# A two-layer DeltaNet and attention backbone: query norms moved to the end of the heads, the output weights' first casts moved to GpSimd, rotation rows placed behind turned blocks, and the last stage's sums read one tile later

## The chip, the cores and the metric

The kernel runs on one NeuronCore of a Trainium2 chip. The metric is the device time of one execution in microseconds (us), from the chip's own clock. PE is the matrix engine, DVE the vector engine, ACT the scalar engine, POOL the GpSimd engine, and SP the queue that issues most DMAs.

## The reference, cut to what matters

512 latent tokens and 256 context tokens of width 1024 go through two layers. Layer 0 is a gated DeltaNet in both directions with 16 value heads, 8 query/key heads and chunks of 64 tokens. Layer 1 is grouped-query attention with rotary positions. A final norm ends it.

```python
def l2_norm(x):
    return x * lax.rsqrt(jnp.sum(x * x, axis=-1, keepdims=True) + NORM_EPS)

# layer 0
qkv = jax.nn.silu(centred_dwconv(p[..., :DN_CONV_DIM], conv_w))   # p = u @ w_in
z   = p[..., DN_CONV_DIM:DN_CONV_DIM + DN_VAL_DIM]
q   = jnp.repeat(l2_norm(q), 2, axis=2)                           # its scale: the query norms
...
def step(s, xs):                                                  # the chunk scan
    v_new = u_i - w_i @ s
    o = qd_i @ s + qk_i @ v_new
    s = s * gl_i + kd_i.T @ v_new
...
y   = (rms_norm(o, o_norm_g) * jax.nn.silu(z)) @ w_out            # output weights
# layer 1
q, k = apply_axial_rope(rms_norm(q, q_norm_g)), apply_axial_rope(rms_norm(k, k_norm_g))
y = (softmax(q @ k.T * d ** -0.5) @ v * jax.nn.silu(z)) @ w_out
# end
h = h + gate * y
out = rms_norm(h, final_norm_g)
```

## The kernel before, in words

Every float32 operand of a large product is split into a high half (a cast to the type fp32r) and a low half (the operand less its high half), and a product takes three passes: high by high, low by high, high by low. A weight's cast therefore has a subtraction behind it, and PE waits for both. The stages, by the trace's clock:

- **Heads**, about 185 to 574 us. Forty slots of input columns (eight q, k pairs, then values `v` and gates `z`) go through a product, a convolution of five taps (L773) and a SiLU (L790, L792), with weights split at L744 and L747. Beside that POOL and DVE solve the triangular systems of the chunks (names `X`, `L`, `tmp`, `df`, `KQ`). The work is a list of `Piece` objects, each with an engine, a cost and a due time. A list scheduler (`written_out`) writes out the order once, when the program is built: it always takes the piece that can start first, and of those the one that is due first. A slot is `SLOT = 8.8` us and there are `N = 40`. One such piece is the **query norms**: eleven small DVE instructions of `rsqrt_steps` (L194 to L202) on the tile `rq` (128x48), the sums of squares of the queries, which the scan uses later.
- **Scan**, about 574 to 752 us. Twelve steps of four parts run as a hand-written loop over `x`; an iteration writes `products(x)`, `solve(x-1)` and `update(x-2)`. `products` has PE make `ks` from the state `S`, DVE make `r` (L1161), ACT make `o` (L1164), and POOL scale `S` (L1167) and add `o` to `O` (L1170). `solve` has PE make `pr` (L1184) from `r` and ACT copy it to `vn` (L1186). `update` has PE make `pq` (L1210) and `su` (L1218), and DVE add them to `O` (L1224) and `S` (L1232). Engines run their instructions in the order of this text, so whatever stands between two of them delays the second. At its end the loop also prepares the output product: fifteen steps that make the norm factors `fo` of the output (the list `chain`: L1086, L194 to L202, L1088), the first scaled copy of the output `so` (`out_scale`, ACT, L1282), and the split of the first output weights: `out_high` (L1267, the cast `woh`, on ACT) and `out_low` (L1274, the low half `wol`, on POOL).
- **Output product**, about 752 to 898 us: 32 units (two groups of tokens by sixteen heads), each with turned, gated and split columns and products into `po` (L1325).
- **Keys and values of layer 1**, about 898 to 945 us. `u_block(k, ...)` has PE turn a block of the normed tokens into a PSUM tile `ht` (L1449), DVE scale it in place (L1454), ACT copy it as the high half and DVE subtract for the low half `uL` (L1456). `kv_block` multiplies the halves by the weights (L1596). There are two such PSUM tiles in turn, so the PE's third `ht` waits for the first `uL`. `rope_rows` prepares the rotation rows with the norms' weights: eight DVE instructions, four of `cg` (L1652) and four of `sg` (L1653), 128x256. POOL meanwhile casts and splits weights for the next stage (`wz`, `wq`; L1565 the cast, L1566 the low half).
- **Attention**, to about 1137 us, and the **tail** to the end: the output product of layer 1 over four tiles of 128 tokens, the gate and residual (`finish_half`, L1987 and L1988), the square sums on ACT (L1989, into `ss`), the final norm (`finish_norm`, L1996 to L2000) and the store. A tile comes in two halves of 512 columns, and DVE reads the square sum of each half before it goes on.

Of the kernel before, what the change touches and what calls it, by code (L numbers as in the profile page):

```python
# [17 lines left out]
P = 128  # L18
# [68 lines left out]
def backbone(tc, a, out):  # L87
# [97 lines left out]
    def rsqrt_steps(x, mul, out=None, room=None):  # L185

        n = x.shape[1]
        rcount[0] += 1
        y, t = (rsp.tile([P, NT * VH], F32, tag=f"rs{i}", name=f"rs{i}_{rcount[0]}")[:, 0:n] for i in range(2))
        if room is not None:  # L190
            t = room
        yi = y.bitcast(I32)
        steps = [
            lambda: V.tensor_scalar(x, x, mul, EPS, ALU.mult, ALU.add),  # L194
            lambda: V.tensor_scalar(yi, x.bitcast(I32), -0.5, float(0x5F3759DF), ALU.mult, ALU.add),
        ]
        for i in range(3):
            to = (x if out is None else out) if i == 2 else y
            steps += [
                lambda: V.scalar_tensor_tensor(t, x, -0.5, y, ALU.mult, ALU.mult),  # L200
                lambda: V.tensor_tensor(t, t, y, ALU.mult),
                lambda to=to: V.scalar_tensor_tensor(to, t, 1.5, y, ALU.add, ALU.mult),  # L202
            ]
        return steps
# [828 lines left out]
    for t, due in enumerate((170, 200, 230, 260, 290, 320)):  # L1033
# [5 lines left out]
        for v in range(2):  # L1039
# [220 lines left out]
            c += m  # L1260
        zs_[n] = z

    def out_high(n):

        gi, h = units0[n]
        wh = fw.tile([P, D], F32R, tag="wh", name=f"woh{h}_{gi}", bufs=3)
        S.copy(wh, raws[n])  # L1267
        halves[n] = [wh]

    def out_low(n):  # L1270

        gi, h = units0[n]
        wl = fw.tile([P, D], F32R, tag="wl", name=f"wol{h}_{gi}", bufs=3)
        G.tensor_tensor(wl, raws.pop(n), halves[n][0], ALU.subtract)  # L1274
# [61 lines left out]
    squares = [(t, h) for t in (1, 0, 5) for h in range(VH)]  # L1336
    for x in range(50):
        if x == 47:
            out_scale(0)
        if x < 48:  # L1340
            products(x)
        if 0 <= x - 1 < 48:
            solve(x - 1)
        if x == 48:
            pt = out_gated(0)
        if x == 49:
            out_product(0, 2)
# [12 lines left out]
        if x in (28, 32, 36, 40):  # L1360
            with tc.issue_after(mark[0]):
                (out_load if x < 36 else gate_load)((x - 28) // 4 % 2)
        if x in (45, 46):
            out_high(x - 45)
        if x in (47, 48):
            out_low(x - 47)
        if x == 47:
            out_load(2)
            out_turn(0)
        if x == 48:  # L1370
            out_rest(0, pt)
            out_scale(1)
# [85 lines left out]
    def u_block(k, j, tiles, dst):  # L1458
        u_split(k, j, u_turn(k, j, tiles), dst)
# [210 lines left out]
    kr = {}  # L1670
# [231 lines left out]
    for u in range(32 + 4):  # L1902
# [33 lines left out]
        for half in range(2):  # L1936
            if piece and piece[0] is q_products:
                q_products(*piece[1:], range(half * 4, half * 4 + 4))
            elif piece:
                k0 = 4 * (u % 2) + 2 * half  # L1940
                z_products(piece[1], range(k0, k0 + 2))
            elif half == 0 and 26 <= u < 33:
                out_block(u - 26, 0, pg)
            elif half == 0 and u >= 33:
                s_all = raw(s3, 0, [[1, 3 * 512]])
                acc1 = [s_all[:, nh * 512:(nh + 1) * 512] for nh in range(2)]
                for k in ((0, 1, 2), (3, 4, 5), ())[u - 33]:
                    out_block(k, 1, acc1)
                if u == 35:
                    out_block(7, 0, pg)  # L1950
            if half == 1 and o is not None:
                q_turned(*last[1:], o)
            if u == 32 and half == 0:
                aq_c.__exit__(None, None, None)
                f2_c = tc.tile_pool(name="fo", bufs=2, side="right", reuse_waits="tile")
                f2 = f2_c.__enter__()
                fg = f2.tile([P, D], F32, tag="fg", name="fg", bufs=1)
                gate1 = f2.tile([P, 1, D], F32, tag="gate1", name="gate1", bufs=1)
                ss = f2.tile([P, 4, 2], F32, tag="ss", name="ss", bufs=1)
# [25 lines left out]
    def finish_half(t, nh, jk):  # L1985
        c = slice(nh * 512, nh * 512 + 512)
        V.tensor_tensor(jk[:, c], acc[t][nh], gate1[:, 0, c], ALU.mult)  # L1987
        V.tensor_tensor(hs[t][:, c], hs[t][:, c], jk[:, c], ALU.add)  # L1988
        S.activation(jk[:, c], hs[t][:, c], AF.Square, accum_out=ss[:, t, nh:nh + 1])  # L1989
        if nh == 0:  # L1990
            V.tensor_scalar(ss[:, t, 0:1], ss[:, t, 0:1], 1.0 / D, EPS, ALU.mult, ALU.add)  # L1991

    def finish_norm(t):

        x, y, w = (f2.tile([P, 1], F32, tag=f"fr{i}", name=f"fr{i}_{t}") for i in range(3))
        V.tensor_scalar(x, ss[:, t, 1:2], 1.0 / D, ss[:, t, 0:1], ALU.mult, ALU.add)  # L1996
        V.tensor_scalar(y.bitcast(I32), x.bitcast(I32), -0.5, float(0x5F3759DF - 0x400000), ALU.mult, ALU.add)  # L1997
        for _ in range(3):
            V.tensor_scalar(w, x, y, y, ALU.mult, ALU.mult)  # L1999
            V.tensor_scalar(y, w, 1.5, y, ALU.subtract, ALU.mult)  # L2000
        return y
# [6 lines left out]
    for t in range(4):  # L2008
        jk = f2.tile([P, D], F32, tag="jko", name=f"jko{t}")
        if t < 3:  # L2010
            for k in range((KT, 6, 0)[t], KT):
                out_block(k, t, acc[t])
            for nh in range(2):
                finish_half(t, nh, jk)
            V.scalar_tensor_tensor(jk, hs[t], finish_norm(t), fg, ALU.mult, ALU.mult)
            send(t, jk, slice(0, D), dma)
            if t == 0:
                load_hs(3)
        else:
            halves_ = [slice(0, 512), slice(512, D)]  # L2020
            hg = wp.tile([P, D], F32, tag="w", name="hg", bufs=3)
            for nh in range(2):
                for k in range(KT):
                    out_block(k, t, acc[t], (nh,))
                finish_half(t, nh, jk)
                V.tensor_tensor(hg[:, halves_[nh]], hs[t][:, halves_[nh]], fg[:, halves_[nh]], ALU.mult)  # L2026
            r = finish_norm(t)
            S.activation(hg[:, halves_[0]], hg[:, halves_[0]], AF.Copy, scale=r)  # L2028
            send(t, hg, halves_[0], nc.scalar.dma_start)
            V.tensor_scalar(hg[:, halves_[1]], hg[:, halves_[1]], r, None, ALU.mult)  # L2030
            send(t, hg, halves_[1], dma)
    written.__exit__(None, None, None)
    f2_c.__exit__(None, None, None)
    at_c.__exit__(None, None, None)
# [31 lines left out]
```

## Time and profile before

| what | value |
|---|---|
| median of 3 runs | 1188.99 us (1187.13 to 1191.74) |
| profiled execution | 1189.06 us, of which the trace's span is 1187.2 us |
| mean granted PE clock | 0.987 |
| PE busy | 1131.2 us, 95% of the span |
| DVE, ACT, POOL busy | 801.9, 721.1 and 584.0 us |

In the trace, a row of a timeline gives the start, the duration, the engine, the line, the operation, the tile written and the tiles read; the bracket at its end gives the time for which the engine stood idle before it and what ended that. A granted clock of 0.5 is half speed. Rows of a window give, per engine, the busy time, then the granted PE clock in the third place from the end.

### The profile page before, as it was taken

Reading aid. Unit: us, or ns where it says so; the run is one execution under the profiler, and the core shown is the slowest. Engines: PE = TensorE matmul, PEld = TensorE weight load, DVE = VectorE, ACT = ScalarE, POOL = GpSimd, SP = SyncE. Lnnn points to the kernel's source line nnn. Section 1 sums busy time; section 2 is a strip of 40 time slices with the busy share of each in tenths; the row PEclk is TensorE's granted clock in tenths of the full one; section 3 lists DMA queues with packets and bytes.
Section 4 is the critical chain, followed back from the end, with each engine's and each line's share of the span. In section 5 each row is a group of like instructions: output and inputs, shape, how many; then the busy total and the mean of one; then the engine's idle time right before and its main releaser. Section 6 shows DMA issues by size and latency. Waiting matters only on the chain. (4 is left out here: it accounts for less than half of the span.)

```text
span 1187.2 us, 27636 instructions
## 1 busy us (share of the span) xinstructions
PE 1131.2 (95%) x10739; PEld 919.0 (77%) x10739; DVE 801.9 (68%) x1723; ACT 721.1 (61%) x1885; POOL 584.0 (49%) x443
## 2 busy tenths in 40 slices
PE   3998999999979999999999999899999999999995
PEld 1676778888868888888666666688887889999884
DVE  2669565889898777763588888546557466667646
ACT  3343333889666873874478998785753246666721
POOL 0130004499998998441285586555744244130900
PEclk9899999999999999999999999999999999999998
DMA  9477976866549544979599996475744112101323
GB/s 332 153 240 240 298 218 187 238 165 167 147 138 284 182 133 131 292 218 286 157 257 248 248 274 162 158 224 185 241 155 134 36 54 72 36 19 54 107 71 89
DMA packets 171124, 208.72 MB, mean 176 GB/s; under 512 B 12497, under 2 KB 126322, under 8 KB 170226
## 3 DMA queue, kind: packets, MB, share of 16 engines
q1 hardware_dynamic: 150914, 195.19, 55.7%
q10 hardware_dynamic: 20080, 11.77, 3.3%
q8 instruction: 85, 1.39, 0.5%
q14 instruction: 45, 0.37, 0.1%
HBM read 166.16 MB, written 40.67 MB: 174 GB/s over the span
## 5 line engine op out<-in xcount | busy, mean ns | idle before, releaser
L1325 PE MATMUL po<-woh,y 128*128 128x512 f32 x384 | 129.3, 401 | 0.7 <-ACT y L1301 0.7
L1167 POOL TENSOR_TENSOR S<-S,glb 128x512 f32<-128x512 f32 x80 | 81.7, 1042 | 70.0 <-PE ks L1158 70.0
L1274 POOL TENSOR_TENSOR wol<-wo,woh 128x1024 fp32r<-128x1024 f32 x32 | 77.1, 2412 | 54.6 <-ACT woh L1267 51.6
L644 POOL TENSOR_TENSOR X<-X,tmp 128x62 f32<-128x62 f32 (+15 forms) x93 | 97.0, 1043 | 7.3
L773 DVE SCALAR_TENSOR_TENSOR acc_v<-g_v,cwv,acc_v 128x510 f32<-128x510 f32 (+3 forms) x128 | 78.2, 615 | 31.9 <-ACT acc_v L765 28.2
L758 PE MATMUL g_v<-uh,wh_v 128*128 128x512 f32 (+1 forms) x256 | 89.4, 349 | 6.6 <-DVE sil_z L790 6.6
L643 POOL TENSOR_TENSOR tmp<-L,X 128x62 f32<-128x62 f32 (+15 forms) x93 | 86.4, 929 | 6.8
L758 PE MATMUL g_z<-uh,wh_z 128*128 128x512 f32 (+1 forms) x256 | 88.7, 346 | 0.0
L758 PE MATMUL g_v<-ul,wh_v 128*128 128x512 f32 (+1 forms) x256 | 87.2, 341 | 0.0
L758 PE MATMUL g_v<-uh,wl_v 128*128 128x512 f32 (+1 forms) x256 | 87.0, 340 | 0.0
L758 PE MATMUL g_z<-ul,wh_z 128*128 128x512 f32 (+1 forms) x256 | 86.6, 338 | 0.4 <-issue 0.4
L758 PE MATMUL g_z<-uh,wl_z 128*128 128x512 f32 (+1 forms) x256 | 86.7, 338 | 0.0
L1325 PEld LDWEIGHTS po<-woh,y 128*128 128x128 f32 x384 | 72.3, 188 | 15.9 <-ACT y L1301 0.9
L1325 PE MATMUL po<-wol,y 128*128 128x512 f32 x192 | 75.6, 394 | 0.9 <-POOL wol L1274 0.9
L333 POOL TENSOR_TENSOR wl_k<-w_k,wh_k 128x1024 fp32r<-128x1024 f32 x8 | 19.1, 2389 | 103.8 <-ACT wh_k L332 103.8
L758 PEld LDWEIGHTS g_v<-uh,wh_v 128*128 128x128 f32 x256 | 49.2, 192 | 12.4 <-DVE sil_z L790 6.9
L1299 DVE SCALAR_TENSOR_TENSOR pt<-pt,og,z 128x128 f32<-128x128 f32 x96 | 34.4, 358 | 34.3 <-PE pt L1290 31.5
L1232 DVE TENSOR_TENSOR S<-su,S 128x512 f32<-128x512 f32 x80 | 51.5, 686 | 6.0 <-PE su L1218 3.9
L1158 PE MATMUL ks<-S,ck 128*64 128x256 f32 x352 | 55.2, 392 | 0.4 <-ACT o L1164 0.4
L758 PEld LDWEIGHTS g_v<-uh,wl_v 128*128 128x128 f32 x256 | 49.2, 192 | 5.5
L758 PEld LDWEIGHTS g_z<-uh,wl_z 128*128 128x128 f32 x256 | 48.9, 191 | 5.7 <-issue 0.5
L758 PEld LDWEIGHTS g_z<-uh,wh_z 128*128 128x128 f32 x256 | 49.0, 192 | 5.3 <-issue 0.4
(432 smaller groups left out, 3342.5 us busy)
## 6 DMA issues: line engine op xcount, KB each, us to landing
aw<-in_ada_w SPq DMA_DIRECT2D x24, 1024.0 KB, 8.3
wo<-in_dn_w_out SPq DMA_DIRECT2D x32, 512.0 KB, 3.4
cv<-v_d SPq DMA_DIRECT2D x48, 256.0 KB, 7.8
w_z<-in_dn_w_in SPq DMA_DIRECT2D x16, 512.0 KB, 5.0
w_v<-in_dn_w_in SPq DMA_DIRECT2D x16, 512.0 KB, 4.6
v_d<-vt ACTq DMA_DIRECT2D x16, 384.0 KB, 4.1
cT<-t_d SPq DMA_DIRECT2D x12, 512.0 KB, 8.3
ckt<-kt_d SPq DMA_DIRECT2D x12, 512.0 KB, 6.6
```

The source lines that it names most:

```text
L333: E.tensor_tensor(wl[:, :, :m], w[:, :, :m], wh[:, :, :m], ALU.subtract)
L643: G.tensor_tensor(tv, bcast(L[:, :, j + 1:, j], 3, j + 1), bcast(X[:, :, j, 0:j + 1], 2, n), ALU.mult)
L644: G.tensor_tensor(X[:, :, j + 1:, 0:j + 1], X[:, :, j + 1:, 0:j + 1], tv, ALU.subtract)
L758: T.matmul(ps[:, :m], w[:, k], u[:, k, c0:c0 + m], start=k == 0 and n_ == 0, stop=k == KT - 1 and n_ == 2)
L773: V.scalar_tensor_tensor(acc[:, c0 + lo:c0 + hi], ps[:, lo + j - 2:hi + j - 2], cwv[:, j, ct:ct + 1], acc[:, c0 + lo:c0 + hi], ALU.mult, A ...
L1158: T.matmul(ks[r0:r0 + 64, w], kq[w][:, hh, r0:r0 + 64], St[hh][:, d], start=True, stop=True)
L1167: G.tensor_tensor(St[hh], St[hh], bcast(g_, 3, P), ALU.mult)
L1232: V.tensor_tensor(St[hh], sj, St[hh], ALU.add)
L1274: G.tensor_tensor(wl, raws.pop(n), halves[n][0], ALU.subtract)
L1299: V.scalar_tensor_tensor(pj, pj, og, raw(z, off, [[st_, 2], [1, 64]]), ALU.mult, ALU.mult)
L1325: T.matmul(acc[:, nh], y[i][:, j, :], ww[k][:, nh * 512:(nh + 1) * 512], start=h == 0 and x == 0, stop=h == VH - 1 and x == 2)
```

## The change

There are four edits. The query norms get a due time 5 us earlier and the condition not to start before the scheduler's time 376. In the scan the steps of `chain` begin one iteration earlier, three per iteration; the first two casts of output weights run on POOL, at x = 44 and 46, each with its subtraction right behind it; and `solve(46)` is written ahead of `out_scale(0)` and `products(47)`. The eight rotation instructions go behind the first two `u_block`s, four each. In the tail each tile's sum is read by DVE after it has begun on the next part, and the last tile comes in parts of 512, 256 and 256 columns.

```diff
-    Piece("DVE", 2.4, N * SLOT, lambda: [f_() for f_ in rsqrt_steps(rq.rearrange("p t h -> p (t h)"), 1.0)], after=[last["rq", h] for h in range(QH)])
+    Piece("DVE", 2.4, N * SLOT - 5, lambda: [f_() for f_ in rsqrt_steps(rq.rearrange("p t h -> p (t h)"), 1.0)], after=[last["rq", h] for h in range(QH)], since=376.0)
...
-    def out_high(n):
+    def out_high(n, E=S.copy):
...
-        S.copy(wh, raws[n])
+        E(wh, raws[n])
...
         if x == 47:
+            solve(x - 1)
             out_scale(0)
         if x < 48:
             products(x)
-        if 0 <= x - 1 < 48:
+        if 0 <= x - 1 < 48 and x != 47:
             solve(x - 1)
...
-        if x in (43, 44, 45):
+        if x in (42, 43, 44, 45):
             some(chain, 3)
         if x == 46:
             some(chain, 99)
...
-        if x in (45, 46):
-            out_high(x - 45)
-        if x in (47, 48):
-            out_low(x - 47)
+        if x in (44, 46):
+            out_high((x - 44) // 2, G.tensor_copy)
+            out_low((x - 44) // 2)
...
-    for w_ in range(2):
-        for s_ in range(2):
-            rope_rows(w_, s_)
     for k in range(6):
         kv_block(k, (0, 1))
     for k in range(2):
         u_block(k, 0, (2, 3, 4, 5), uL)
+        rope_rows(0, k)
+        rope_rows(1, k)
...
+    CHUNKS = [((0, 512), (512, 512))] * 3 + [((0, 512), (512, 256), (768, 256))]
...
+    finish_part(0, 0)
+    finish_part(0, 1)
+    finish_sum(0, 0)
+    finish_part(1, 0)
+    r = finish_row(0)
+    finish_part(1, 1)
+    finish_sent(0, r)
...
+    finish_part(2, 0)
+    finish_part(2, 1)
+    finish_sum(2, 0)
+    r = finish_row(2)
+    finish_part(3, 0)
+    finish_sent(2, r)
+    weighed(0)
+    finish_sum(3, 0)
+    finish_part(3, 1)
+    weighed(1)
+    finish_sum(3, 1)
+    finish_part(3, 2)
+    weighed(2)
+    finish_sum(3, 2)
+    r = finish_norm(3)
```

`finish_part` is the gate, the residual and the ACT square of one part; `finish_sum` reads that part's square sum; `finish_row` is the last sum and the norm; `finish_sent` is the scaling and the store.

DVE's order in the heads, before: the query norms (`rq`, with `rs` as scratch) stand behind the low half of a weight and ahead of the two SiLUs `sil_z` of a gate slot, of which the first is shown.

```order
L194 TENSOR_SCALAR rq<-rq 128x48
L195 TENSOR_SCALAR rs_10_3908<-rq 128x48
L200 TENSOR_SCALAR rs_10_3909<-rq,rs_10_3908 128x48
L201 TENSOR_TENSOR rs_10_3909<-rs_10_3909,rs_10_3908 128x48
L202 TENSOR_SCALAR rs_10_3908<-rs_10_3909,rs_10_3908 128x48
L200 TENSOR_SCALAR rs_10_3909<-rq,rs_10_3908 128x48
L201 TENSOR_TENSOR rs_10_3909<-rs_10_3909,rs_10_3908 128x48
L202 TENSOR_SCALAR rs_10_3908<-rs_10_3909,rs_10_3908 128x48
L200 TENSOR_SCALAR rs_10_3909<-rq,rs_10_3908 128x48
L201 TENSOR_TENSOR rs_10_3909<-rs_10_3909,rs_10_3908 128x48
L202 TENSOR_SCALAR rq<-rs_10_3909,rs_10_3908 128x48
L790 TENSOR_SCALAR sil_z_3906<-sil_z_3906,g_z_3756 128x512
```

DVE's order after, 173 rows further on, near the end of the heads:

```order
L790 TENSOR_SCALAR sil_z_6861<-sil_z_6861,g_z_6784 128x512
L194 TENSOR_SCALAR rq<-rq 128x48
L195 TENSOR_SCALAR rs_10_6890<-rq 128x48
L200 TENSOR_SCALAR rs_10_6891<-rq,rs_10_6890 128x48
L201 TENSOR_TENSOR rs_10_6891<-rs_10_6891,rs_10_6890 128x48
L202 TENSOR_SCALAR rs_10_6890<-rs_10_6891,rs_10_6890 128x48
L200 TENSOR_SCALAR rs_10_6891<-rq,rs_10_6890 128x48
L201 TENSOR_TENSOR rs_10_6891<-rs_10_6891,rs_10_6890 128x48
L202 TENSOR_SCALAR rs_10_6890<-rs_10_6891,rs_10_6890 128x48
L200 TENSOR_SCALAR rs_10_6891<-rq,rs_10_6890 128x48
L201 TENSOR_TENSOR rs_10_6891<-rs_10_6891,rs_10_6890 128x48
L202 TENSOR_SCALAR rq<-rs_10_6891,rs_10_6890 128x48
```

All eleven instructions have moved there; the SiLU that stood behind them now stands right behind that low half, and otherwise the order of the heads on DVE, PE, ACT and POOL is the same. On SP one store of a `sil_z` goes behind two loads of the scan's first step.

POOL's order at the end of the scan, before: the last four additions to `O`, then the low halves of the first output weights.

```order
L1170 TENSOR_TENSOR O_7019<-O_7019,o_9750 128x512
L1170 TENSOR_TENSOR O_7019<-O_7019,o_9811 128x512
L1170 TENSOR_TENSOR O_7019<-O_7019,o_9869 128x512
L1170 TENSOR_TENSOR O_7019<-O_7019,o_9923 128x512
L1274 TENSOR_TENSOR wol_0_9964<-wo_0_8748,woh_0_9866 128x1024
L1274 TENSOR_TENSOR wol_0_9999<-wo_0_9009,woh_0_9916 128x1024
```

POOL's order after, at the same place:

```order
L1170 TENSOR_TENSOR O_7019<-O_7019,o_9753 128x512
L1267 COPY woh_0_9813<-wo_0_8748 128x1024
L1274 TENSOR_TENSOR wol_0_9815<-wo_0_8748,woh_0_9813 128x1024
L1170 TENSOR_TENSOR O_7019<-O_7019,o_9818 128x512
L1170 TENSOR_TENSOR O_7019<-O_7019,o_9874 128x512
L1267 COPY woh_0_9918<-wo_0_9009 128x1024
L1274 TENSOR_TENSOR wol_0_9920<-wo_0_9009,woh_0_9918 128x1024
L1170 TENSOR_TENSOR O_7019<-O_7019,o_9938 128x512
```

A cast and its subtraction now stand between the first and the second of these additions, and again ahead of the last.

DVE's order at the start of the keys and values, before: all eight rotation instructions stand ahead of the first block.

```order
L1652 TENSOR_SCALAR cg_11583<-rope,qg 128x4x64
L1653 TENSOR_SCALAR sg_11585<-rope,qg 128x4x64
L1652 TENSOR_SCALAR cg_11583<-rope,qg 128x4x64
L1653 TENSOR_SCALAR sg_11585<-rope,qg 128x4x64
L1652 TENSOR_SCALAR cg_11584<-rope,qg 128x4x64
L1653 TENSOR_SCALAR sg_11586<-rope,qg 128x4x64
L1652 TENSOR_SCALAR cg_11584<-rope,qg 128x4x64
L1653 TENSOR_SCALAR sg_11586<-rope,qg 128x4x64
L1454 TENSOR_SCALAR ht_0_11682<-ht_0_11682,au_81 128x512
L1456 TENSOR_TENSOR uL_11591<-ht_0_11682,uL_11590 128x512
L1454 TENSOR_SCALAR ht_0_11690<-ht_0_11690,au_81 128x512
```

DVE's order after, at the same place:

```order
L1454 TENSOR_SCALAR ht_0_11674<-ht_0_11674,au_81 128x512
L1456 TENSOR_TENSOR uL_11591<-ht_0_11674,uL_11590 128x512
L1652 TENSOR_SCALAR cg_11583<-rope,qg 128x4x64
L1653 TENSOR_SCALAR sg_11585<-rope,qg 128x4x64
L1652 TENSOR_SCALAR cg_11584<-rope,qg 128x4x64
L1653 TENSOR_SCALAR sg_11586<-rope,qg 128x4x64
L1454 TENSOR_SCALAR ht_0_11686<-ht_0_11686,au_81 128x512
L1456 TENSOR_TENSOR uL_11591<-ht_0_11686,uL_11590 128x512
L1652 TENSOR_SCALAR cg_11583<-rope,qg 128x4x64
L1653 TENSOR_SCALAR sg_11585<-rope,qg 128x4x64
L1652 TENSOR_SCALAR cg_11584<-rope,qg 128x4x64
L1653 TENSOR_SCALAR sg_11586<-rope,qg 128x4x64
```

The first block's `ht` and `uL` have moved ahead of the rotation instructions, and the second and the third block each stand behind four of them.

More of the change, by code (lines that the diff above doesn't have):

```diff
@@ L1958, in backbone @@
                 gate1 = f2.tile([P, 1, D], F32, tag="gate1", name="gate1", bufs=1)
-                ss = f2.tile([P, 4, 2], F32, tag="ss", name="ss", bufs=1)
+                ss = f2.tile([P, 4, 3], F32, tag="ss", name="ss", bufs=1)
                 dma(gate1, gate_d[1])
@@ L1983, in backbone, with out_chunk, finish_part, finish_sum @@
     acc = [pg, acc1, [tr_tile(f"pso2{nh}").rearrange("p a b -> p (a b)") for nh in range(2)], [s_all[:, 1024:1536], po]]
-    def finish_half(t, nh, jk):
-        c = slice(nh * 512, nh * 512 + 512)
-        V.tensor_tensor(jk[:, c], acc[t][nh], gate1[:, 0, c], ALU.mult)
+    jks = [f2.tile([P, D], F32, tag="jko", name=f"jko{t}") for t in range(2)]
+    CHUNKS = [((0, 512), (512, 512))] * 3 + [((0, 512), (512, 256), (768, 256))]
+    def out_chunk(k, t, c0, n):
+        cc_, (bank, b0) = slice(c0, c0 + n), divmod(c0, 512)
+        for x, (i, j) in enumerate(PASS):
+            T.matmul(acc[t][bank][:, b0:b0 + n], yT[i][:, k, t * P:(t + 1) * P], wo[j][:, k, cc_], start=k == 0 and x == 0, stop=k == KT - 1 and x == 2)
+    def finish_part(t, i):
+        c0, n = CHUNKS[t][i]
+        c, (bank, b0) = slice(c0, c0 + n), divmod(c0, 512)
+        jk = jks[t]
+        V.tensor_tensor(jk[:, c], acc[t][bank][:, b0:b0 + n], gate1[:, 0, c], ALU.mult)
         V.tensor_tensor(hs[t][:, c], hs[t][:, c], jk[:, c], ALU.add)
-        S.activation(jk[:, c], hs[t][:, c], AF.Square, accum_out=ss[:, t, nh:nh + 1])
-        if nh == 0:
+        S.activation(jk[:, c], hs[t][:, c], AF.Square, accum_out=ss[:, t, i:i + 1])
+    def finish_sum(t, i):
+        if i == 0:
             V.tensor_scalar(ss[:, t, 0:1], ss[:, t, 0:1], 1.0 / D, EPS, ALU.mult, ALU.add)
+        else:
+            V.tensor_scalar(ss[:, t, 0:1], ss[:, t, i:i + 1], 1.0 / D, ss[:, t, 0:1], ALU.mult, ALU.add)
     def finish_norm(t):
-        x, y, w = (f2.tile([P, 1], F32, tag=f"fr{i}", name=f"fr{i}_{t}") for i in range(3))
-        V.tensor_scalar(x, ss[:, t, 1:2], 1.0 / D, ss[:, t, 0:1], ALU.mult, ALU.add)
+        x = ss[:, t, 0:1]
+        y, w = (f2.tile([P, 1], F32, tag=f"fr{i}", name=f"fr{i}_{t}") for i in range(2))
         V.tensor_scalar(y.bitcast(I32), x.bitcast(I32), -0.5, float(0x5F3759DF - 0x400000), ALU.mult, ALU.add)
@@ L2006, in send @@
             q(out[0, c_ * 64:c_ * 64 + 64, c], x[hf * 64:hf * 64 + 64, c])
[L2008 to L2031, printed above, removed]
@@ new lines, in finish_row, with finish_sent @@
+    def finish_row(t):
+        finish_sum(t, 1)
+        r = finish_norm(t)
+        return r
+    def finish_sent(t, r):
+        V.scalar_tensor_tensor(jks[t], hs[t], r, fg, ALU.mult, ALU.mult)
+        send(t, jks[t], slice(0, D), dma)
+    for k in (6, 7):
+        out_block(k, 1, acc[1])
+    for t in (2, 3):
+        for c0, n in CHUNKS[t]:
+            for k in range(KT):
+                out_chunk(k, t, c0, n)
+    finish_part(0, 0)
+    finish_part(0, 1)
+    finish_sum(0, 0)
+    finish_part(1, 0)
@@ new lines, in backbone, with weighed @@
+    r = finish_row(0)
+    finish_part(1, 1)
+    finish_sent(0, r)
+    load_hs(3)
+    finish_sum(1, 0)
+    r = finish_row(1)
+    finish_sent(1, r)
+    jks += [f2.tile([P, D], F32, tag="jko", name=f"jko{t}") for t in (2, 3)]
+    hg = wp.tile([P, D], F32, tag="w", name="hg", bufs=3)
+    def weighed(i):
+        c0, n = CHUNKS[3][i]
+        V.tensor_tensor(hg[:, c0:c0 + n], hs[3][:, c0:c0 + n], fg[:, c0:c0 + n], ALU.mult)
+    finish_part(2, 0)
+    finish_part(2, 1)
+    finish_sum(2, 0)
@@ L2032, in backbone @@
+    r = finish_row(2)
[10 more added lines that the diff above has]
+    r = finish_norm(3)
+    S.activation(hg[:, 0:512], hg[:, 0:512], AF.Copy, scale=r)
+    send(3, hg, slice(0, 512), nc.scalar.dma_start)
+    V.tensor_scalar(hg[:, 512:], hg[:, 512:], r, None, ALU.mult)
+    send(3, hg, slice(512, D), dma)
     written.__exit__(None, None, None)
```

## The prediction

> **What bounds the kernel now.** I read the engine shares and the granted clock on the page first, then PE's waits, then the timelines around the four places.
>
> ```profile
> PE 1131.2 (95%) x10739; PEld 919.0 (77%) x10739; DVE 801.9 (68%) x1723; ACT 721.1 (61%) x1885; POOL 584.0 (49%) x443
> PEclk9899999999999999999999999999999999999998
> ```
>
> PE is busy for 95% of the span and its clock is nearly always full. So an edit changes the time only where it makes or removes idle time of PE, where it changes PE's clock, or behind PE's last instruction. The waits of PE that bear on this change:
>
> ```profile
> PE g_v L758 <- DVE sil_z L790: 6.6, 1, 6.6
> PE G L595 <- DMA kq_0m<-k_d: 2.0, 1, 2.0
> PE ht L1449 <- DVE uL L1456: 1.3, 2, 1.1
> ```
>
> Only the first is long, and it is the one behind the query norms. Two behaviours of the chip decide the sizes. One is seen where a small DVE instruction meets a POOL instruction (DVE, POOL, DVE):
>
> ```profile
> 742.97 1.27 DVE L200 SCALAR_TENSOR_TENSOR rs<-fo,rs 128x48 f32<-128x48 f32 x1
> 742.90 1.28 POOL L1170 TENSOR_TENSOR O<-O,o 128x512 f32<-128x512 f32 x1 [2.52 <-ACT o L1164]
> 744.28 0.21 DVE L201 TENSOR_TENSOR rs<-rs,rs 128x48 f32<-128x48 f32 x1
> ```
>
> The DVE instruction reads two tiles of SBUF, starts 0.07 us behind POOL's and lasts 1.27 us, until POOL's has ended; its neighbour of the same size takes 0.21. I call this being blocked. The other is PE's clock after a wait (two windows):
>
> ```profile
> 200.30:203.70 3.40, 3.38 (x43) 3.21 (x44) 0.88 (x2) 0.00 (x0) 0.52 (x1) 0.51 0.90 204
> 355.00:360.00 5.00, 5.00 (x12) 3.86 (x13) 4.89 (x6) 0.60 (x1) 4.69 (x5) 0.50 0.85 280
> ```
>
> Behind the wait of 2.0 us (the `G` above) PE ran at 0.51 of its clock for 3.4 us; behind the one of 6.6 us it was still at 0.50 some 5 us later.
>
> **Query norms.** PE, DVE, POOL around the old place, and the new place at the end:
>
> ```profile
> 339.79 1.21 DVE L194 TENSOR_SCALAR rq<-rq 128x48 f32<-128x48 f32 x1
> 352.94 1.15 DVE L202 SCALAR_TENSOR_TENSOR rq<-rs,rs 128x48 f32<-128x48 f32 x1
> 354.73 0.79 PE L758 MATMUL g_v<-uh,wh_v 128*128 128x512 f32 x1 [6.63 <-DVE sil_z L790]
> 363.17 1.15 PE L712 MATMUL GQ<-kq_1q 128*64 128x64 f32 x32
> 1169.46 5.76 PE L1845 MATMUL po<-wo,yT 128*128 128x512 f32 x24
> 365.22 4.77 POOL L545 TENSOR_TENSOR df_1q<-df_1q,KQ 128x1024 f32<-128x1024 f32 x2 [4.11 <-DVE KQ L721]
> 466.52 5.75 POOL L545 TENSOR_TENSOR df_2q<-df_2q,KQ 128x1024 f32<-128x1024 f32 x2
> 481.22 0.68 DVE L792 SCALAR_TENSOR_TENSOR sil_v<-g_v,acc_v 128x512 f32<-128x512 f32 x1
> 485.47 0.40 PE L758 MATMUL g_z<-uh,wh_z 128*128 128x512 f32 x1
> 581.53 2.04 POOL L1167 TENSOR_TENSOR S<-S,glb 128x512 f32<-128x512 f32 x2 [30.11 <-PE ks L1158]
> 567.29 1.02 DVE L790 SCALAR_TENSOR_TENSOR sil_z<-sil_z,g_z 128x512 f32<-128x512 f32 x2 [9.93 <-ACT sil_z L781]
> ```
>
> The eleven instructions run from 339.79 to 354.09, 14.3 us, because POOL solves beside them and most are blocked in turn. At about 0.21 each they would take 2.3. PE loses the wait of 6.63 and then the clock: 24 matmuls take from 354.73 to 363.17, 8.44 us, where 24 of the same size take about 5.6 (the fifth row, less its overlap). That is 2.8, so 9.4 together. At the new place POOL is idle for 30 us and DVE for 9.9, so they cost nothing; without that cover they would cost at most the 14.3 of now. On SP the store that now goes behind two loads is read only in the output product. What of the 9.4 stays? DVE's `KQ` can come earlier and take POOL's idle 4.11 before 365.22. From 370.0 to 466.5 I found no idle POOL worth naming, so its solve ends only 4.1 earlier, and DVE's weighing of `X` behind it, in front of a dense DVE. PE needs a PSUM bank freed by `sil_v` (ends 481.90) for the product at 485.47: it has 3.6 us of room there and, at the next such place, about 2. So PE can gain between 4.1 + 2 and 4.1 + 3.6. I take 6.0; the ends are 4, if no room passes, and 9.4.
>
> **End of the scan.** ACT, POOL, DVE, then PE:
>
> ```profile
> 739.36 1.08 ACT L1267 CAST woh<-wo 128x1024 fp32r<-128x1024 f32 x1
> 735.16 1.28 POOL L1170 TENSOR_TENSOR O<-O,o 128x512 f32<-128x512 f32 x1 [2.80 <-ACT o L1164]
> 748.30 4.69 POOL L1274 TENSOR_TENSOR wol<-wo,woh 128x1024 fp32r<-128x1024 f32 x2
> 737.16 1.12 DVE L1161 SCALAR_TENSOR_TENSOR r<-ks,negV,cv 128x128 f32<-128x128 f32 x4
> 746.53 0.55 PE L1290 MATMUL pt<-ident,so 128*128 128x128 f32 x3 [1.20 <-ACT o L1164]
> 750.71 0.50 PE L1325 MATMUL po<-wol,y 128*128 128x512 f32 x1 [0.86 <-POOL wol L1274]
> ```
>
> What can be gained are PE's two waits shown, 2.1, of which the casts taken off ACT and the earlier `wol` reach perhaps half: 1. Against it: at x = 44 POOL adds to `O` until 736.44, and the moved cast (1.0 to 1.1, as on ACT; POOL's own is in the next part) and subtraction (4.69 / 2 = 2.35) follow until about 740.0. DVE's three steps of the chain, 0.2 each when free, stand right ahead of `r` at 737.16, so from about 736.5. The first is blocked by the cast, one or two more by the subtraction. So `r` starts near 740.3 instead of 737.16, 3.2 later. Queued behind it on DVE are the additions to `O` and `S`, and PE waits for `r` (`pr`) and then for ACT's `o`. PE idles about 3 us, and the clock may halve, as after 2.0 above, which costs 1.5. Some is regained, because the steps no longer stand at x = 46 all together and `solve(46)` is ahead of `products(47)`. I take +4.0: the delay of 3.2 and half of the clock's price. The ends are -1 (DVE's steps get through before POOL's) and +6.5 (3.2 with the whole clock, and 1.3 to 1.8 more at x = 42 and 46, where the steps meet POOL's `S` and `O`, 1.28).
>
> The Trainium skill, in "TensorE: Matmul & The Clock Gate", Part 1: The HAM clock gate, says that the clock halves after at least one idle window of about 3.4 us and returns after about 3.4 us of work. The trace agrees on the 3.4 us of half clock behind the wait of 2.0, but that wait was shorter than a window and the wait of 6.6 kept PE at half for longer than one. By the page's rule the 3 us here would leave the clock full, this part would be +3.2 and the whole sum 0.8 lower; the longer wait below would still halve it.
>
> **Rotation rows.** PE, DVE and POOL at the start of layer 1's keys and values:
>
> ```profile
> 907.09 2.21 PE L1449 MATMUL ht<-dn,h 128*128 128x128 f32 x16 [0.50 <-issue]
> 917.33 1.13 PE L1449 MATMUL ht<-dn,h 128*128 128x128 f32 x8 [0.21 <-DVE uL L1456]
> 906.80 1.26 DVE L1653 SCALAR_TENSOR_TENSOR sg<-rope,qg 128x256 f32<-128x256 f32 x1
> 907.98 0.41 DVE L1652 SCALAR_TENSOR_TENSOR cg<-rope,qg 128x256 f32<-128x256 f32 x1
> 910.84 0.81 DVE L1454 TENSOR_SCALAR ht<-ht,au 128x512 f32<-128x512 f32 x1
> 916.49 0.69 DVE L1456 TENSOR_TENSOR uL<-ht,uL 128x512 fp32r<-128x512 f32 x1 [0.65 <-ACT uL L1455]
> 909.28 1.36 POOL L1565 CAST wq<-w1q 128x1024 fp32r<-128x1024 f32 x1 [1.50 <-DMA w1q<-in_att_w_in]
> 910.60 2.54 POOL L1566 TENSOR_TENSOR wz<-w1z,wz 128x1024 fp32r<-128x1024 f32 x1
> 913.11 2.38 POOL L1566 TENSOR_TENSOR wq<-w1q,wq 128x1024 fp32r<-128x1024 f32 x1
> ```
>
> Before, the eight instructions end at 910.84, two of them blocked by casts (1.26 against 0.41). Then the three blocks follow every 2.1 us and the third `uL` ends at 917.18, for which PE's next `ht` waits 0.21. After, the first `ht` is ready with PE's turn at about 908.2 and its `uL` ends at 910.4 (0.81, 0.65 for ACT, 0.69). The next four instructions now run beside POOL's two subtractions, which last from 910.60 to 915.49 and block two of them: they end at about 916.5, where four free ones of 0.41 would end at 912. The second `uL` then ends at 918.7, the next four at about 920.0 to 920.9 (other casts of POOL run there), the third `uL` at about 922. PE has work until 917.1 and its next `ht` starts at 922, 4.7 later. The half clock costs up to 2.8, as at 354.73; I take 1.3 of it, since the wait is 4.7 and not 6.6: +6.0. The ends are -1.3 (PE's two waits of 1.3 in all vanish and nothing is blocked) and +9 (4.7 + 2.8, and 1.5 more if casts block all of the second four).
>
> **Tail.** DVE's wait for ACT, its last part, and ACT's last instruction:
>
> ```profile
> 1155.79 0.21 DVE L1996 TENSOR_SCALAR fr<-ss 128x1 f32<-128x1 f32 x1 [0.79 <-ACT jko L1989]
> 1177.72 0.68 DVE L1987 TENSOR_TENSOR jko<-po,gate 128x512 f32<-128x512 f32 x1
> 1179.92 0.21 DVE L1996 TENSOR_SCALAR fr<-ss 128x1 f32<-128x1 f32 x1
> 1182.09 0.72 ACT L2028 ACTIVATE hg<-hg,fr 128x512 f32<-128x512 f32 x1 [2.20 <-DVE fr L2000]
> ```
>
> PE's last product ends at 1175.22 (1169.46 + 5.76), but DVE begins on it only at 1177.72: it is late by its waits for ACT, two of 0.79 in each of three tiles, 4.7. Without them it waits for PE instead. The last part then starts at 1175.3 with 256 columns: 0.4 + 0.4 on DVE, 0.6 on ACT, 0.2 for the sum and 1.9 for the norm (from 1180.17 to 1182.03 now), and 0.4 of handing over: ACT's instruction starts at 1179.2, 2.9 earlier. The store behind it stays. The ends are -2 (the shorter matmuls are less efficient, a tile waits for its buffer) and -3.2.
>
> The sum: -6.0 + 4.0 + 6.0 - 2.9 = +1.1. From the profiled execution's 1189.06 that is 1190.2; it lies 0.07 above the median, so I say 1190.1.
>
> **The rivals.** *The blocking goes the other way (faster).* If DVE's steps start ahead of POOL's casts by a fraction of a microsecond, POOL waits and DVE is not blocked; POOL's idle 2.8 ahead of 735.16 and 1.50 ahead of 909.28 can hide that. Then -6.0 - 1 - 1.3 - 2.9 = -11.2: 1177.9. For it: the starts, 736.44 and about 736.5, lie close together. Against: POOL's subtractions are long and next to each other at 910.60 to 915.49. The Trainium skill, in "SBUF — State Buffer", Who interferes with whom, says the same of the shared port: issue order decides who blocks.
>
> *PE's clock falls at both new waits (slower).* Where the waits are longer than about 2 us, the shortest that halves the clock in this trace, both pay in full: -6.0 + 6.5 + 9 - 2.9 = +6.6, 1195.7, and 1197.7 if the norms give only 4. For it: both estimated waits, 3 and 4.7, lie above that point. Against: each must happen as long as I estimate.
>
> *The whole 9.4 of the norms passes through.* If DVE's later room is larger than read, -9.4 + 4.0 + 6.0 - 2.9 = -2.3: 1186.8. For it: PE's other waits in the heads are short. Against: POOL's solve.
>
> That the change does not do what it says is excluded by the order.
>
> **How the numbers follow.** About 0.5%, 5.9 us, is what a measurement of this kernel can tell from no change. My case has 0.48, its own range 1185 to 1195 from the ends of its terms; blocking the other way 0.20; the clock 0.24; the whole gain of the norms 0.08. Faster by over 0.5% (below 1183): the first rival and the low ends of my case, 0.20 + 0.04 = 0.24. Slower by over 0.5% (above 1194.9): most of the clock's case and the high ends of mine, 0.20 + 0.06 = 0.26. The rest, 0.50, is in between. The range reaches to the middle of both outer cases: 1177 to 1199.
>
> **What would show each step.** The norms: PE's wait of 6.6 at 354.7 and the half clock behind it are gone, POOL's wait for `KQ` is shorter, and the scan starts 6 us earlier. The scan: three DVE steps of over 1 us ahead of one `r`, PE idle for 3 us at x = 45. The rotation rows: two `sg` or `cg` of 2 us or more and PE idle for over 4 us before the third `ht`. The tail: no 0.79 ahead of the sums, DVE waiting for PE, 2.9 less from PE's last matmul to the end. It is wrong if DVE's small steps pass unblocked at x = 44, or if the scan starts more than 8 us earlier.

## The result, and the profile after

The changed kernel takes 1204.19 us (median of 4 runs, 1201.66 to 1207.19) against 1188.18 (1187.13 to 1191.74) for the kernel before: a ratio of 1.013, 95% interval 1.0098 to 1.0163. It is 16 us slower. I had forecast 1190.1 and a range up to 1199.

The page of the changed kernel, shares and clock (a digit is the granted clock in a fortieth of the span, in tenths):

```profile
PE 1133.5 (94%) x10763; PEld 921.8 (77%) x10763; DVE 800.3 (67%) x1727; ACT 720.1 (60%) x1885; POOL 588.2 (49%) x445
PEclk9899999999999999999999999999998999999996
```

PE's busy time has grown by only 2.3 (1131.2 before), so some 13 of the 15.2 us by which the span grew (1202.4 against 1187.2) are idle time. PE's waits (us in total, times, the longest):

```profile
PE ht L1449 <- DVE uL L1456: 6.8, 1, 6.8
PE g_z L758 <- DVE sil_v L792: 3.7, 2, 3.4
PE ks L1158 <- ACT o L1164: 3.4, 2, 2.7
PE pr L1184 <- ACT vn L1186: 3.0, 2, 1.7
```

The wait of 6.6 at the query norms is gone and these have come or grown. But none of them is at the end, where most of the time went. To see where, I took the start of the same matmul in both traces and subtracted. The columns are places by the time of before; a minus is a lead over the profiled execution of before (us):

| kernel | 337, ahead of the norms | 573, scan begins | 765, output product | 935, keys and values | 1152, last tiles | end of span |
|---|---|---|---|---|---|---|
| changed | -0.9 | -5.5 | -3.3 | +4.0 | +3.8 | +15.3 |

So the norms gave 4.6, the end of the scan cost 2.2, the rotation rows cost 7.3, and the tail cost 11.5 where I had it gain 2.9. DVE and PE in the tail of the changed kernel:

```profile
1157.74 0.15 DVE L2002 TENSOR_SCALAR ss<-ss 128x1 f32<-128x1 f32 x1
1173.42 0.69 DVE L1996 TENSOR_TENSOR jko<-s,gate 128x512 f32<-128x512 f32 x1 [15.53 <-PE s L1990]
...
1153.62 2.96 PE L1844 MATMUL s<-wo,yT 128*128 128x512 f32 x12
1167.62 5.76 PE L1990 MATMUL s<-wo,yT 128*128 128x512 f32 x24
1173.22 5.83 PE L1990 MATMUL po<-wo,yT 128*128 128x256 f32 x48
...
1197.34 0.72 ACT L2069 ACTIVATE hg<-hg,fr 128x512 f32<-128x512 f32 x1 [2.20 <-DVE fr L2013]
```

DVE stands for 15.53 us before it reads tile 1's first half, which PE had finished at 1156.58 (1153.62 + 2.96), and starts when PE has ended the last tile's first half: 1167.62 + 5.76 = 1173.38. Both lie in one PSUM tile of three banks, `s`: tile 1 in its first two, the last tile's first half in the third. In the new text all matmuls of the last tile stand ahead of the reads of tile 1: the loop that writes them stands in lines that the diff above skips, right ahead of `finish_part(0, 0)`, and the first experiment's edit shows it. Before, they stood behind those reads, and the same read had no wait (DVE):

```profile
1159.19 0.68 DVE L1987 TENSOR_TENSOR jko<-s,gate 128x512 f32<-128x512 f32 x1
```

Three tiles of DVE work are then still to do behind PE's last product but one, and the end comes 18.3 us after PE's last matmul (1179.05) with ACT's last instruction, where it was 6.9 before.

### The profile page after: what moved, and what is told of

It is laid out like the page before. It is cut to its first block, busy times and chain, and to the rows that moved or that the text cites. A ratio compares the mean times of both kernels' runs of the same rounds, so it can differ in the third digit from the quotient of the medians.

```text
span 1202.4 us, 27692 instructions
## 1 busy us (share of the span) xinstructions
PE 1133.5 (94%) x10763; PEld 921.8 (77%) x10763; DVE 800.3 (67%) x1727; ACT 720.1 (60%) x1885; POOL 588.2 (49%) x445
## 4 chain that ended last, share of the span: by engine, by line
PE 68%; POOL 15%; DVE 9%; DMA 4%; issue 2%; ACT 1%; SPq 0%; POOLq 0%; ACTq 0%; DVEq 0%
PE po L1325 11%; PE ks L1158 6%; POOL X L644 6%; PE g_z L758 6%; POOL tmp L643 6%; PE g_k L343 4%; PE pg L1710 3%; PE g_q L758 3%; PE pg L1761 3%; PE su L1218 3%; PE po L1830 3%; PE g_v L758 3%; PE s L1781 3%; PE kv L1596 2%; PE pr L1184 2%
## 5 line engine op out<-in xcount | busy, mean ns | idle before, releaser
L758 PEld LDWEIGHTS g_z<-ul,wh_z 128*128 128x128 f32 x256 | 49.7, 194 | 5.0 <-issue 0.2
L1161 DVE SCALAR_TENSOR_TENSOR r<-ks,negV,cv 128x128 f32<-128x128 f32 x176 | 52.0, 343 | 2.0 <-PE ks L1158 1.1
```

The costliest lines, as they stand in the source:

```text
L758: T.matmul(ps[:, :m], w[:, k], u[:, k, c0:c0 + m], start=k == 0 and n_ == 0, stop=k == KT - 1 and n_ == 2)
L1161: V.scalar_tensor_tensor(r[:, 2 * j + i], ks[:, 0, i], negV[:, visit, t, h:h + 1], v[:, h], ALU.mult, ALU.add)
```

## The experiments

The times scatter more here than above: the kernel before ranged from 1185.56 to 1203.69 us in one set of runs and from 1187.76 to 1197.57 in the other. Ratios are to its runs in the same set, and the small terms are read from the table below, which takes each kernel's own trace.

**The last tile's matmuls moved in the text.** It undoes only that part of the tail's edit (`out_chunks(t)` is the removed inner loop for one tile).

```diff
-    for t in (2, 3):
-        for c0, n in CHUNKS[t]:
-            for k in range(KT):
-                out_chunk(k, t, c0, n)
+    out_chunks(2)
     finish_part(0, 0)
...
     finish_part(1, 1)
+    out_chunks(3)
     finish_sent(0, r)
```

> The changed kernel, with only the place in the text moved at which the last tile's matmuls are written: behind the reads of tile 1, as before the change. The instructions' order on each engine is the same. Theory 1: DVE's first read of tile 1 waits until PE has written everything of the three-bank PSUM tile that stands ahead of that read in the text, which since the change includes the last tile's first half. Then the wait of 15.5 us goes, the tail takes my forecast of 2.9 less than before the change, and the time is 1204.2 - 11.4 - 2.9 = about 1190 (1188 to 1192). Rival: the new order of sums, the two output buffers or the shorter matmuls make the tail late; then it stays within 3 of 1204.

Measured: 1.0008 (0.9985 to 1.0031) of the kernel before, from 1.013. DVE, PE and ACT in its tail:

```profile
1160.95 0.68 DVE L1996 TENSOR_TENSOR jko<-s,gate 128x512 f32<-128x512 f32 x1
1182.23 0.42 DVE L1996 TENSOR_TENSOR jko<-po,gate 128x256 f32<-128x256 f32 x1 [1.22 <-PE po L1990]
1183.82 0.41 DVE L1996 TENSOR_TENSOR jko<-po,gate 128x256 f32<-128x256 f32 x1
...
1176.36 5.83 PE L1990 MATMUL po<-wo,yT 128*128 128x256 f32 x48
...
1187.44 0.72 ACT L2072 ACTIVATE hg<-hg,fr 128x512 f32<-128x512 f32 x1 [2.20 <-DVE fr L2013]
```

The wait of 15.5 is gone. The tail now gains 1.5 over before, not 2.9, for the same reason on a smaller scale: both last parts of 256 columns lie in the tile `po`, and the first waits until PE has written the second (1176.36 + 5.83 = 1182.19), though its own matmuls are the first half of that row. Whether the tile or the bank decides cannot be told there, since `po` is one bank.

**The last tile's banks exchanged.**

```diff
-    acc = [pg, acc1, [... pso2 ...], [s_all[:, 1024:1536], po]]
+    acc = [pg, acc1, [... pso2 ...], [po, s_all[:, 1024:1536]]]
```

> The changed kernel, with the last tile's two PSUM banks exchanged: its first 512 columns go to the single bank, its last 512 to the third bank of the three-bank tile that tile 1 also uses. Theory 1: DVE's first read of tile 1 now waits for PE's very last matmul, 5.8 us later than in the changed kernel: 1204.2 + 5.5 = about 1209.5. Rival (lateness of the order itself): no change, 1204.

Measured: 1209.93 us, 1.0153 (1.0109 to 1.0197) of the kernel before. That interval also holds the changed kernel's 1.013, so the times alone do not decide against the rival. The trace does: from 1152 to the end (table below) the tail costs 17.2, against 11.5 in the changed kernel. DVE's wait and PE's last matmuls:

```profile
1177.04 0.69 DVE L1996 TENSOR_TENSOR jko<-s,gate 128x512 f32<-128x512 f32 x1 [21.20 <-PE s L1990]
...
1171.17 5.83 PE L1990 MATMUL s<-wo,yT 128*128 128x256 f32 x48
```

With the last columns in `s`, DVE waits 21.20 instead of 15.53, until PE's very last matmul (1177.00). No instruction's order changed, only which bank shares the tile. That settles the cause: the wait follows the tile as a whole, and the order of the text.

**The query norms alone.** The first hunk of the change on the kernel before.

```diff
-    Piece("DVE", 2.4, N * SLOT, ...)
+    Piece("DVE", 2.4, N * SLOT - 5, ..., since=376.0)
```

> The kernel before, with only the query norms moved. If the four parts add up as the two traces show them at their stages: -5.5, 1182.7 (1181.5 to 1184). Rival: the 9.4 that PE gains at the old place is taken back only because of other parts of the change; then about 1179.

Measured: 0.9952 (0.9917 to 0.9988), 5.7 us less. The interval would also hold the rival's 9.4; the trace decides, with a gain of 5.5 up to the start of the scan (from +0.2 to -5.3), as expected. At the end the lead is 1.4, because this execution then lost 1.8 in the middle of the scan and 2.4 at its end (both below).

**The end of the scan alone.** All its hunks on the kernel before.

```diff
-        if x in (45, 46):
-            out_high(x - 45)
-        if x in (47, 48):
-            out_low(x - 47)
+        if x in (44, 46):
+            out_high((x - 44) // 2, G.tensor_copy)
+            out_low((x - 44) // 2)
...
```

> The kernel before, with only the edits at the end of the scan. From the two traces, PE enters that stage 5.5 early and leaves it 3.2 early, so +2.3: 1190.5 (1189 to 1192), with `r` of x = 45 held up some 3 us by two chain steps beside POOL's cast and subtraction. Rival, my forecast with a halved clock: +4.0, 1192.

Measured: 0.9984 (0.9964 to 1.0004), not the +2.3 expected, so no difference that can be told. Its own trace does lose about 2.5 from 728 to 765 against the one of before; why the times do not show it is taken up with the prediction's steps. DVE, POOL and PE show the mechanism all the same:

```profile
737.12 0.95 DVE L200 SCALAR_TENSOR_TENSOR rs<-fo,rs 128x48 f32<-128x48 f32 x1
738.10 2.39 DVE L201 TENSOR_TENSOR rs<-rs,rs 128x48 f32<-128x48 f32 x1
740.41 1.11 DVE L1161 SCALAR_TENSOR_TENSOR r<-ks,negV,cv 128x128 f32<-128x128 f32 x4
...
736.96 1.04 POOL L1267 CAST woh<-wo 128x1024 fp32r<-128x1024 f32 x1
738.08 2.34 POOL L1274 TENSOR_TENSOR wol<-wo,woh 128x1024 fp32r<-128x1024 f32 x1
...
741.80 0.65 PE L1158 MATMUL ks<-S,ck 128*64 128x256 f32 x4 [2.65 <-ACT o L1164]
742.72 1.07 PE L1158 MATMUL ks<-S,ck 128*64 128x256 f32 x4
```

One chain step lasts as long as POOL's cast and the next as long as its subtraction; `r` waits behind them and PE 2.65 for `o`.

**Rotation rows without POOL's subtractions.** On the kernel with the matmuls moved in the text; `whole` is false for the first `wq` and the first two `wz`.

```diff
-            G.tensor_tensor(dst[1][:, k0:k0 + m], wv, dst[0][:, k0:k0 + m], ALU.subtract)
+            if whole:
+                G.tensor_tensor(dst[1][:, k0:k0 + m], wv, dst[0][:, k0:k0 + m], ALU.subtract)
+            else:
+                G.memset(dst[1][:, k0:k0 + m].bitcast(F32), 0.0)
```

> The kernel of the run with the matmuls moved in the text, in which POOL's subtractions for the first weights of layer 1 (wz, wq) are left out and their low halves set to zero earlier, so that these heads get a coarser product; POOL's casts stay. The order of DVE's instructions is unchanged, and the rotation rows stand behind the first two blocks. Theory 1: what makes the rotation rows cost 7 us is that they are blocked by these subtractions. Then cg and sg take 0.4 each (1.3 beside a cast), PE's wait of 6.8 for the third block goes to under 1 and the time is 5 below the kernel before. Rival: four more instructions between the blocks are enough to make PE wait; then the wait stays over 4 and the time 0 to +2 above the kernel before.

Measured: 0.9968 (0.9946 to 0.9990). DVE, POOL and PE:

```profile
906.46 0.42 DVE L1655 SCALAR_TENSOR_TENSOR cg<-rope,qg 128x256 f32<-128x256 f32 x1
910.54 1.26 DVE L1655 SCALAR_TENSOR_TENSOR cg<-rope,qg 128x256 f32<-128x256 f32 x1
...
910.48 1.06 POOL L1565 CAST wz<-w1z 128x1024 fp32r<-128x1024 f32 x1 [1.69 <-DMA w1z<-in_att_w_in]
...
914.36 1.13 PE L1449 MATMUL ht<-dn,h 128*128 128x128 f32 x8 [2.73 <-DVE uL L1456]
```

Seven of eight take 0.4, one is blocked by a cast. The stage costs 1.1 (from -4.1 to -3.0) instead of 7.3, so 6.2 came from the subtractions, the half clock behind the longer wait included. I expected the wait to go below 1 and missed: it is still 2.73, because the eight instructions, 3.3 us together and 0.8 of blocking, do delay the third block. The rival had a small part of it.

**A version that beats both.** The norms; the tail with the matmuls moved and the last 256 columns in a bank that tile 0 has left; the rotation rows behind the whole loop of blocks; the end of the scan as before.

```diff
     for k in range(KT):
         ...
+    for w_ in range(2):
+        for s_ in range(2):
+            rope_rows(w_, s_)
...
+        if (t, c0) == (3, 768):
+            return pg[0][:, 0:n]
```

> The kernel before with the query norms moved, the tail's new order with the last tile's matmuls written behind the reads of tile 1 and its last 256 columns in a bank that tile 0 has left, and the rotation rows behind the whole loop of blocks, where the trace of before has POOL idle for 22 us and DVE for 5.5. Nothing of the end of the scan is changed. Sum of the stages: -5.5 (norms), -1.6 (tail, as measured with the matmuls moved) and up to -1.6 more for the last part's own bank, -1.3 (PE's two waits for uL): about 10 below the kernel before (8 to 11). Rival: the rotation rows' new place delays the first keys; then 3 to 6 below.

Measured: 1181.15 us, 0.9905 (0.9876 to 0.9935) of the kernel before, 11 us faster. DVE among the rotation rows and at the part in `po`, PE's last matmuls and ACT's last instruction:

```profile
933.37 0.42 DVE L1652 SCALAR_TENSOR_TENSOR cg<-rope,qg 128x256 f32<-128x256 f32 x1
935.71 0.42 DVE L1653 SCALAR_TENSOR_TENSOR sg<-rope,qg 128x256 f32<-128x256 f32 x1
...
1169.66 0.41 DVE L2002 TENSOR_TENSOR jko<-po,gate 128x256 f32<-128x256 f32 x1
...
1168.11 3.00 PE L1996 MATMUL pg<-wo,yT 128*128 128x256 f32 x24
...
1174.87 0.72 ACT L2078 ACTIVATE hg<-hg,fr 128x512 f32<-128x512 f32 x1 [2.21 <-DVE fr L2019]
```

All eight run unblocked where POOL is idle, and the stage gains 1.8. DVE reads the part in `po` while PE still writes the last one in `pg`. ACT's last instruction starts 3.76 after PE's last matmul (1171.11) instead of 6.87: 3.1 gained there (2.8 by the span), about what I had forecast for the tail.

**`solve(46)` first, alone.** That one edit added to the version above.

```diff
         if x == 47:
+            solve(x - 1)
             out_scale(0)
...
-        if 0 <= x - 1 < 48:
+        if 0 <= x - 1 < 48 and x != 47:
```

> As the run with norms, tail and late rotation rows, and in addition only the one edit at the end of the scan that writes solve(46) ahead of out_scale(0) and products(47); chain and casts as before the change. If it is this edit that regained PE's time behind x = 45 (2.7 us in the changed kernel's trace), 1 to 2.7 less than without it: 11 to 12.5 below the kernel before. Rival: the regained time came from the earlier casts and subtractions, then no difference.

Measured: 0.9926 (0.9896 to 0.9955), no better than without it, as the rival had it. From 728 to 765 it loses 1.2, as the version above does. PE no longer waits 1.19 for `o` there, but 1.36 for `vn`, and 1.54 instead of 0.89 for `wol`:

```profile
741.92 0.67 PE L1184 MATMUL pr<-r,cT 64*64 64x128 f32 x16 [1.36 <-ACT vn L1186]
```

**No chain step at x = 44.** All edits at the end of the scan, on the version above.

```diff
-        if x in (42, 43, 44, 45):
-            some(chain, 3)
+        if x in (42, 43, 45):
+            some(chain, 4)
```

> As the run with norms, tail and late rotation rows, with all the edits at the end of the scan, but with no chain step at x = 44, where POOL casts and subtracts (four steps each at x = 42, 43 and 45, the rest at 46). Theory 1: two chain steps beside the cast and subtraction cost PE its wait of 2.65 for o. Then that wait goes, and the stage comes out 0.5 or more faster than before the change: about 10.5 to 11 below the kernel before. Rival: r or o is late for another reason, such as POOL's additions coming late; then the wait of 2.65 stays and the time is 8 below.

Measured: 0.9919 (0.9894 to 0.9945), between the two expectations. DVE, POOL and PE:

```profile
741.77 1.20 DVE L202 SCALAR_TENSOR_TENSOR rs<-rs,rs 128x48 f32<-128x48 f32 x1
...
741.63 1.27 POOL L1170 TENSOR_TENSOR O<-O,o 128x512 f32<-128x512 f32 x1
...
740.18 0.65 PE L1158 MATMUL ks<-S,ck 128*64 128x256 f32 x4
745.76 1.13 PE L1184 MATMUL pr<-r,cT 64*64 64x128 f32 x16 [2.59 <-ACT vn L1186]
```

PE's wait of 2.65 for `o` is gone (`ks` at 740.18 has none), as theory 1 said, but the stage still costs 2.1. A step now meets POOL's addition, which the cast and subtraction have pushed back, and with `solve(46)` first PE waits 2.59 for `vn`. The wait moved by one part of the scan.

PE's lead by stage, as in the first table; 728 lies ahead of the edits at the end of the scan:

| kernel | 337 | 573 | 728 | 765 | 935 | 1152 | end |
|---|---|---|---|---|---|---|---|
| changed | -0.9 | -5.5 | -5.5 | -3.3 | +4.0 | +3.8 | +15.3 |
| matmuls moved in the text | +2.5 | -2.3 | -2.2 | -0.1 | +7.1 | +6.9 | +5.4 |
| banks exchanged | -3.5 | -10.3 | -7.6 | -5.5 | +2.0 | +1.7 | +18.9 |
| norms alone | +0.2 | -5.3 | -3.5 | -1.1 | -1.1 | -1.4 | -1.4 |
| end of the scan alone | -2.3 | -3.3 | -0.9 | +1.6 | +1.6 | +1.4 | +1.5 |
| without subtractions | -1.6 | -7.9 | -6.2 | -4.1 | -3.0 | -3.2 | -4.8 |
| version that beats both | -3.0 | -9.9 | -3.3 | -2.1 | -3.9 | -4.2 | -7.0 |
| with solve(46) first | -0.6 | -5.1 | -1.4 | -0.2 | -2.0 | -2.3 | -4.4 |
| no chain step at 44 | +1.2 | -5.0 | 0.0 | +2.1 | +0.3 | 0.0 | -2.9 |

## Why the prediction was wrong, by its own steps

**The tail** is the step that failed. I wrote -2.9 with ends of -2 and -3.2, and named a buffer and shorter matmuls as the worst. Measured: +11.5. I costed the new order from DVE's and ACT's instructions, and took PE's end as the only thing DVE could wait for. I did not ask, for each read that the new text puts behind a later matmul, whether the two share a PSUM tile. Exchanging the banks and moving the matmuls show that this wait is the whole error: without it, and with the last part in a bank of its own, the tail gives 2.8 to 3.1. The buffer that I named as the worst did make DVE wait, 1.71 with the matmuls moved and 1.53 in the version that beats both, and one wait of 0.73 for ACT is left, but all but some 0.1 of that is hidden behind PE's matmuls. Also wrong is the line that DVE would be waiting for PE's end: it was, but 5.7 us before that end and with three tiles still to do.

**The other three terms** came out near in size against the trace of before; together they give +4.9, where I had +4.0.

- Query norms: -6.0 forecast, -4.6 in the changed kernel, -4.5 to -6.9 over eight traces. PE's lead of 9.6 behind the old place is taken back at waits for `sil_v`, as I said, in the changed kernel at the one that I named: PE waits there 3.38 (first row, PE), just what my 9.4 less 6.0 leaves. What my sum left out is the clock behind that wait, at half for 3.4 us (second row, 0.76 as the mean of 7 us). It splits the eight traces: the four with a half clock behind a wait for `sil_v` gain 4.5 to 5.5, the four without it 6.2 to 6.9. Some of that is scatter of the executions: the end of the scan alone, which leaves the norms in place, gains 1.0 over the same stretch. The eleven instructions take 2.6 at their new place (last two rows, DVE):

```profile
478.60 0.50 PE L758 MATMUL g_z<-uh,wh_z 128*128 128x512 f32 x1 [3.38 <-DVE sil_v L792]
...
478.00:485.00 7.00, 6.40 (x21) 5.10 (x22) 6.77 (x13) 6.83 (x21) 4.20 (x2) 0.76 0.98 276
...
550.44 0.18 DVE L194 TENSOR_SCALAR rq<-rq 128x48 f32<-128x48 f32 x1
552.83 0.21 DVE L202 SCALAR_TENSOR_TENSOR rq<-rs,rs 128x48 f32<-128x48 f32 x1
```

- End of the scan: +4.0 forecast, +2.2. The blocking and a wait of 2.65 came as said, with two blocked steps (0.95 and 2.39 us) where I had three. PE lost more than I took, 5.1, with two more waits of 0.77 and 1.70, and regained more behind it, 2.9. Even the 2.2 is against a lucky trace. The norms alone and the version that beats both leave this stage as it was and lose 2.4 and 1.2 there (from 728 to 765): behind the same five waits, of 0.36 to 1.2, their clock fell, and that of before did not (before, norms alone, version that beats both):

```profile
745.00:752.00 7.00, 3.79 (x55) 2.31 (x45) 3.91 (x11) 4.32 (x13) 4.92 (x3) 1.00 0.18 38
745.00:752.00 7.00, 5.41 (x35) 3.57 (x28) 2.16 (x4) 2.75 (x6) 4.87 (x3) 0.63 0.53 171
745.00:752.00 7.00, 5.41 (x42) 3.47 (x34) 2.06 (x5) 2.89 (x6) 4.71 (x4) 0.76 0.51 160
```

So the edit costs between -0.2 and 2.2: its sign is open, and the times (0.9984 for it alone) do not show a cost.

- Rotation rows: +6.0 forecast, +7.3. DVE, POOL and PE in the changed kernel:

```profile
907.29 2.34 DVE L1652 SCALAR_TENSOR_TENSOR cg<-rope,qg 128x256 f32<-128x256 f32 x1
909.56 2.62 DVE L1653 SCALAR_TENSOR_TENSOR sg<-rope,qg 128x256 f32<-128x256 f32 x1
...
906.97 2.39 POOL L1566 TENSOR_TENSOR wz<-w1z,wz 128x1024 fp32r<-128x1024 f32 x1
909.31 2.58 POOL L1566 TENSOR_TENSOR wq<-w1q,wq 128x1024 fp32r<-128x1024 f32 x1
...
919.32 2.05 PE L1449 MATMUL ht<-dn,h 128*128 128x128 f32 x8 [6.84 <-DVE uL L1456]
```

Two instructions are blocked for the length of the two subtractions, as forecast; PE waits 6.84 where I had 4.7: the third `uL` comes when I said, but PE reaches that point earlier, since its wait of 1.1 for the second `ht` is gone. The Trainium skill, in "SBUF — State Buffer", Who interferes with whom, says that a DVE instruction with two SBUF inputs contends with a GpSimd instruction that reads SBUF; the run without subtractions agrees, 0.42 against 2.34 to 2.62.

**The rivals.** Blocking the other way made neither stage cheap in any trace. The clock did fall at the wait of 6.84 (0.50 from 919.3 to 923.5) and not at the one of 2.65, but that is not what made the kernel slow. Of the norms' 9.4 at most 6.9 passed through. The slower outcome had a cause that was on no list of mine.

## What to carry to other kernels

When code is rewritten so that more matmuls stand ahead of an epilogue, go through the reads one by one and ask which later writes share their PSUM tile: in these runs a read through a view into a tile of three banks waited for all of the tile's writes that stood ahead in the text, also those of another bank. Giving each part that is read early a tile of its own, or writing its read ahead of the next write, cost nothing here and was worth 13 us. Small DVE instructions with two SBUF operands belong where POOL is idle; beside POOL's long subtractions they cost 6 of the 7 us of that stage.

## What the runs showed of the hardware that I had not expected

The clock after a short wait is not decided by the wait's length. The same wait of 2.65 for `o` halved the clock in the kernel with the end of the scan alone (`ks` of 1.07 at 742.72) and not in the changed kernel (PE):

```profile
737.11 0.65 PE L1158 MATMUL ks<-S,ck 128*64 128x256 f32 x4 [2.65 <-ACT o L1164]
737.60 0.60 PE L1158 MATMUL ks<-S,cq 128*64 128x256 f32 x4
```

The Trainium skill, in "TensorE: Matmul & The Clock Gate", Part 1: The HAM clock gate, says that the activity window is free-running, so that its phase differs from run to run. These two traces agree with that; its rule that a whole window of about 3.4 us must be idle does not hold here, since 2.65 was enough once. In the heads a shorter wait even did what a longer one did not: behind 1.77 for `sil_v` the clock was 0.50 from 482.9 to 486.3 with the matmuls moved, and behind 2.95 it stayed at 1.00 in the version that beats both.

Seven of the traces also have stops of PE in the middle of the scan, 1.2 to 4.1 us in all, which the trace puts down to "issue" and to no engine; the traces of before, of the changed kernel and of the one with the matmuls moved have none there. They come at different places in each execution, and are at least a part of why leads shrink between 573 and 728. The DMA records of the same traces point at a cause: the queue q8, marked "instruction", moves 16 KB about every 7 us there, once for some 250 instructions of PE (matmuls and weight loads together), and each of the 13 stops ends 1.3 to 1.8 us after such a load has landed. That fits a PE that waits for its next instructions. No run changed those loads, so it is not shown.
